# Sums of w_down in units of 256 columns, in two buffers, loaded by the SP queue

## The chip, the cores and the metric

The kernel runs on one core of one Trainium2 chip. The metric is the device time of one execution in microseconds (us), lower is better; the times shown are medians over several runs. One further execution was taken by the hardware profiler, and its trace is what this text reads. Engines: PE multiplies matrices (PEld loads its weights), DVE, ACT and POOL work on vectors, SP only issues transfers (DMAs). Each engine runs its instructions strictly in its own order; waits between engines, and for transfers, go through semaphores.

## The reference

One layer of a streaming encoder on x of 1024 positions by 1024 features, float32:

```python
h   = rmsnorm(x, norm1_g);  proj = h @ w_in                # q, k, v, forget logits, lru_x, lru_gate
att = forgetting_attention(q, k, v, cumsum(log f))         # 8 heads, causal
rec = rg_lru(conv(lru_x)) * gelu(lru_gate)
x   = x + concat(rmsnorm(att), rmsnorm(rec)) @ w_out
h2  = rmsnorm(x, norm2_g)
x   = x + (silu(h2 @ w_gate) * (h2 @ w_up)) @ w_down       # w_gate, w_up 1024x2816; w_down 2816x1024
```

The change touches the last line alone: the feed-forward part.

## The kernel before, in words

Float32 products are made of three products of split operands: `split` (L72 on ACT makes the high part h, L73 on DVE the low part l), and then h·h, h·l and l·h on PE.

The products with w_gate and w_up use a scheme with seven block products in place of eight. The work goes in 20 **steps**: gate step n and up step n for n = 1 to 10 (n = 0 is done with plain products before). This text calls them g1, u1, g2, u2 and so on. A step is seven **products** numbered 0 to 6, each of 12 matmuls (L936), so 140 products in all. `Step.run` gives products 0, 2, 4 and 6 the same PSUM bank (`x_`), products 1 and 5 another (`z_`), and product 3 a third (`w_`). Products 0, 1 and 2 are copied out by ACT (L1111). Then `result` adds: product 4 is added to the copy of product 1 by DVE, on L1104 in a gate step (`g<-Pg,pug`) and on L1099 in an up step (`puu<-Pu,puu`). Product 6 adds into the bank of product 4, so PE cannot begin it before DVE has read product 4. Between the two lies only product 5.

After each product a hook `after(i)` runs. It makes the operand of the next step that belongs to the same place (POOL sums L1068 to L1071 of raw weights, then `split`), and it carries the sums of w_down:

- `load_wd(f)` loads, for f = 0 to 10, four blocks of w_down (two blocks of rows, two halves of 512 columns each) into the tile `wd` of 128 x 4 x 512, in two transfers of 512 KB issued by ACT (L1019). There is one buffer under the tag `wd`.
- `sum_wd(f, m)`, m = 0 to 3, is one subtraction of 128x512 on DVE (L1025). After m = 3, SP stores the tile to `td[f]` in DRAM (1 MB, L1027). m = 0 reads only what the first transfer brought, m = 1 needs both.
- 13 products in the code are one turn: the load at place 0, the sums at places 7 to 10. The next load into the one buffer must wait until the store before it has landed.

The same tag `wd` is used before the steps by `t_sums` (four 512-column temporaries for every second of four sums). The raw weights of the steps come in pieces of 128x4x256 (512 KB, rows of 1 KB) on SP (`graw`, `uraw`, L901). SP also stores the results g (`gd`, L924) and their differences (`sd`, L928). The last part of the kernel (L1353, products P1 to P7) reads `td`, `sd` and `gd` back.

A scheduler of the framework puts the instructions of each engine into an order of its own, by its estimates of times. So what stands in an engine's order, not what stands in the code, says where a sum or a load comes.

Of the kernel before, what the change touches and what calls it, by code (L numbers as in the profile page):

```python
# [9 lines left out]
F32 = mybir.dt.float32  # L10
# [9 lines left out]
P = 128  # L20
# [14 lines left out]
def hymba_layer(ctx: ExitStack, tc: tile.TileContext, x, norm1_g, w_in, q_norm_g, k_norm_g, b_f,  # L35
# [5 lines left out]
    act, dve, pool, pe, sp = nc.scalar, nc.vector, nc.gpsimd, nc.tensor, nc.sync  # L41
# [18 lines left out]
    def bank(tag, name):  # L60
        return psp.tile([P, 512], F32, tag=tag, name=name, bufs=BANKS[tag])
# [3 lines left out]
    def any_bank(name, tags=("st", "st", "st", "o", "o", "mx")):  # L65
        cyc[0] += 1
        return bank(tags[cyc[0] % len(tags)], name)

    def split(src, h, l, gain=None):

        if gain is None:
            act.copy(out=h, in_=src)  # L72
            dve.tensor_sub(out=l, in0=src, in1=f32(h))  # L73
        else:
            act.activation(out=h, in_=src, func=AF.Copy, scale=gain)
            dve.scalar_tensor_tensor(out=l, in0=src, scalar=gain, in1=f32(h), op0=ALU.mult, op1=ALU.subtract)  # L76

    def rstd(out_t, ss, n, neghalf):

        dve.tensor_scalar(out=out_t, in0=ss, scalar1=1.0 / n, scalar2=EPS, op0=ALU.mult, op1=ALU.add)  # L80
        pool.tensor_tensor(out=out_t, in0=out_t, in1=neghalf, op=ALU.pow)
# [12 lines left out]
    def hs(half):  # L94
        return slice(half * 512, (half + 1) * 512)
# [212 lines left out]
    def sumsq_to_rstd(sq, dst, n, ps, b0=0, b1=NB):  # L308
        for b in range(b0, b1):
            pe.matmul(ps[:, b:b + 1], sq[:, b * P:(b + 1) * P], ones1[:, 0:1], start=True, stop=True)  # L310
        rstd_newton(dst[:, b0:b1], ps[:, b0:b1], n, b1 - b0)

    with tc.tile_pool(name="pp", bufs=1) as pp:
# [99 lines left out]
        for g, src in ((0, w_a), (1, w_x)):  # L413
            for o in range(2):
                sp.dma_start(out=wgr[o * HD:(o + 1) * HD, g, :, o * HD:(o + 1) * HD],
                             in_=src[0].rearrange("(t two) d e -> two d t e", two=2)[o])
# [437 lines left out]
    def mm_out(groups):  # L854

        for kc in range(4):
            wh, wl = woa[kc]
            for ps, b, half in groups:
                bh, bl = atth[kc][:, b * P:(b + 1) * P], attl[kc][:, b * P:(b + 1) * P]
                for m, (a, r) in enumerate(((bh, wh), (bl, wh), (bh, wl))):  # L860
                    pe.matmul(ps, a, r[:, hs(half)], start=(kc == 0 and m == 0), stop=(kc == 3 and m == 2))  # L861
# [35 lines left out]
    def load_raw(nm, n):  # L897
        src = w_gate if nm == "g" else w_up
        for j in range(2):
            raw = slot("v%d" % (2 * (nm == "u") + j), f"{nm}raw{n}{j}", F32, (P, 4, 256))  # L900
            sp.dma_start(out=raw, in_=src[0, j * 512:(j + 1) * 512, n * 256:(n + 1) * 256].rearrange("(k p) c -> p k c", p=P))  # L901
            raws[nm, j] = raw
# [16 lines left out]
    def g_tiles(n):  # L919
        gts[n] = [slot("x%d" % (2 * (n % 2) + i), f"g{n}{i}") for i in range(2)]  # L920
# [18 lines left out]
    def classic(nm, i, half, ops):  # L939
        ps = any_bank(f"c{nm}{i}{half}", A4)  # L940
        for j in range(2):
            product(ps, ops[nm, i, j], B[j, half], j == 0, j == 1)
        g = gts[0][i][:, hs(half)]
        if nm == "g":
            act.activation(out=g, in_=ps, func=AF.Silu)
        else:
            dve.tensor_mul(out=g, in0=g, in1=ps)
# [3 lines left out]
    def classic_ops(i):  # L951
        for nm in "gu":
            for j in range(2):
                ops0[nm, i, j] = make_op(blk(nm, i, j), f"c{nm}{i}{j}")

    with tc.tile_pool(name="nz", bufs=1) as nz:
        g2 = nz.tile([P, D], F32, name="g2")
        sp.dma_start(out=g2, in_=norm2_g[0:1, :].broadcast_to([P, D]))
        for b in range(4, NB):
            sp.dma_start(out=x1[b], in_=x1d[b * P:(b + 1) * P, :])  # L960
        x2d = dr.tile([S, D], F32, name="x2d")

        def norm2_block(b):
            xn = nz.tile([P, D], F32, tag="xn", name=f"x2n{b}", bufs=1)
            act.activation(out=xn, in_=x1[b], func=AF.Square, accum_out=ss2[:, b:b + 1])
            rstd(rs2[:, b:b + 1], ss2[:, b:b + 1], D, neghalf[:, 0:1])
            dve.scalar_tensor_tensor(out=xn, in0=x1[b], scalar=rs2[:, b:b + 1], in1=g2, op0=ALU.mult, op1=ALU.mult)
            ts = slice((b % 4) * P, (b % 4 + 1) * P)
            for kg in range(4):
                ps = any_bank(f"t2{b}{kg}", A4)  # L970
                for j in range(2):
                    kc = kg * 2 + j
                    pe.transpose(ps[:, j * P:(j + 1) * P], xn[:, kc * P:(kc + 1) * P], ident)
                h, l = (t[kg % 2][:, :, ts] for t in B[kg // 2, b // 4])
                split(ps[:, :256].rearrange("p (k t) -> p k t", k=2), h, l)

        for b0, nb in ((0, 2), (2, 1), (3, 1), (4, 1), (5, 1), (6, 1), (7, 1)):
            groups = [(any_bank(f"wa{b}{half}", B4), b, half) for b in range(b0, b0 + nb) for half in range(2)]
            mm_out(groups)
            if b0 in (0, 3):  # L980
                sumsq_to_rstd(sqA, rsA, AW, bank("tr", f"ssA{b0}"), *((0, 4) if b0 == 0 else (4, 8)))
            for ps, b, half in groups:
                dve.scalar_tensor_tensor(out=x1[b][:, hs(half)], in0=ps, scalar=rsA[:, b:b + 1], in1=x1[b][:, hs(half)], op0=ALU.mult, op1=ALU.add)
            for b in range(b0, b0 + nb):
                sp.dma_start(out=x2d[b * P:(b + 1) * P, :], in_=x1[b])
            for b in ((0, 1) if b0 == 2 else (b0 - 1,) if b0 else ()):
                norm2_block(b)
            if b0 == 5:
                load_raw("g", 0)
                load_raw("u", 0)  # L990
            if b0 == 6:
                classic_ops(0)
        g_tiles(0)


        seq = ("o1 g00 N7 ta0 g10 rw tb0 ta1 g11 tb1 ta2 g01 tb2 ta3 mk0 u00 tb3 mk1 u01 mk2 u10 sp0 mk3 mk4 u11 mk5 sp1 "
               "mk6 wd0").split()
        i7 = seq.index("N7")
        for q in seq[:i7]:
            classic_ops(1) if q == "o1" else classic(q[0], int(q[1]), int(q[2]), ops0)  # L1000
        norm2_block(7)

    tz = ctx.enter_context(tc.tile_pool(name="tz", bufs=1))

    def temp(name):
        return tz.tile([P, 512], F32, tag="sf", name=name, bufs=4)


    ND = NFT // 2
    TD = {"T1": 0, "T3": 1, "T4": 2, "T2": 3}  # L1010
    td = dr.tile([ND, P, 4, 512], F32, name="td")
    sd = dr.tile([ND, P, 512], F32, name="sd")
    wds = {}

    def load_wd(f):
        wds[f] = wd = tz.tile([P, 4, 512], F32, tag="wd", name=f"wd{f}", bufs=1)
        for i in range(2):
            rows = slice((ND * i + f) * P, (ND * i + f + 1) * P)
            act.dma_start(out=wd[:, 2 * i:2 * i + 2, :], in_=w_down[0, rows, :].rearrange("p (j c) -> p j c", j=2))  # L1019

    def sum_wd(f, m):

        wd = wds[f]
        o, a, b = ((0, 1, 0), (1, 3, 1), (3, 3, 0), (2, 2, 3))[m]
        dve.tensor_sub(out=wd[:, o, :], in0=wd[:, a, :], in1=wd[:, b, :])  # L1025
        if m == 3:
            sp.dma_start(out=td[f], in_=wd)  # L1027

    T1 = slots4("q", "T1")
    T2 = slots4("k", "T2")  # L1030
# [8 lines left out]
    def t_sums(k):  # L1039

        if k % 2 == 0:
            t = tz.tile([P, 4, 512], F32, tag="wd", name=f"ts{k}", bufs=1)
            u = [t[:, i, :] for i in range(4)]
        else:
            u = [temp(f"ts{k}{i}") for i in range(4)]
        for i, blk_ in enumerate((B11, B12, B21, B22)):
            h, l = ck(blk_, k)
            dve.tensor_add(out=u[i], in0=f32(h), in1=f32(l))
        for o, x_, y_ in ((0, 1, 0), (1, 3, 1), (3, 3, 0), (2, 2, 3)):
            dve.tensor_sub(out=u[o], in0=u[x_], in1=u[y_])  # L1050
        tsum[k] = u
# [199 lines left out]

    for k, st in enumerate(steps):
        def after(i):
            f, m = divmod(7 * k + i + 1, 13)
            if 0 <= f < ND:
                if m == 0:
                    load_wd(f)
                elif 7 <= m < 11:
                    sum_wd(f, m - 7)
            if k + 1 < len(steps):  # L1260
                steps[k + 1].make(i)
            else:
                end_step(i)
        if st.n + 1 < NPR:
            load_raw(st.nm, st.n + 1)
        st.run(after)
# [34 lines left out]
    for n, (nm, a_, b_, pos) in enumerate(dsteps):  # L1301
# [16 lines left out]
        if nm == "P6" and 7 <= pos < 11:  # L1318
            b = pos - 7
# [19 lines left out]
        if nm == "P4" and 4 <= pos < 8:  # L1339
            b = pos - 4  # L1340
# [8 lines left out]
        for b in range(4):  # L1349
# [9 lines left out]
            u = at({"P1": x2t[0, 0], "P2": x2t[0, 0], "P3": val.get("a"), "P7": val.get("q"), "P4": val.get("q")}[nm], b)  # L1359
# [30 lines left out]
```

## Time and profile before

| | us |
|---|---|
| median of three runs | 1179.3 (1174.34, 1179.3, 1183.54) |
| the profiled execution | 1176.27 |
| its span, first to last instruction | 1174.5 |
| PE busy in it | 1140.3 |
| the 20 steps in it, 566.21 to 961.23 | 395.02 |

The profiled execution is 1.77 us longer than its span, and 3.0 us below the median. Its row groups stand below under "Rows read from the trace". Times in them are us from the start of the span. A window row lists its stretch, its length, the busy time of the engine with the instructions in brackets, the granted clock as a share of full speed, the share of the DMA engines' time, and GB/s. A timeline row lists start, length, engine, line, operation, what is written and read, and in square brackets how long the engine stood idle before it and what ended that.

### The profile page before, as it was taken

To read this page: it belongs to the slowest core of one execution; us is meant where nothing else is said; L and a number is where in the kernel's file an instruction comes from. 1 tells how busy PE (TensorE), PEld (TensorE's weight loads), DVE (VectorE), ACT (ScalarE), POOL (GpSimd) and SP (SyncE) were. 2 spreads that over 40 slices of the span, in tenths; PEclk is the share of its full clock that TensorE was granted. 3 is DMA by queue.
4 is the path that set the end of the run, shared out by engine and by line. 5 is a ranking of instruction groups with operands and counts; after the bars stand their busy time and mean duration, and the time that the engine had idled before them with its cause. 6 is when DMAs were issued, how large, how long until landed. Compare 5 with 4: busy or idle time off the path is not lost.

```text
span 1174.5 us, 16494 instructions
## 1 busy us (share of the span) xinstructions
PE 1140.3 (97%) x6137; PEld 966.3 (82%) x6137; DVE 764.4 (65%) x1309; ACT 526.1 (45%) x951; POOL 174.5 (15%) x152
## 2 busy tenths in 40 slices
PE   8999999998999898999989999999999999999998
PEld 7988999996888786778868878888888888888887
DVE  6436858768787875779666665654433446679693
ACT  7427766326464554454333323333333334444442
POOL 2000010012010202000522223232222100000000
PEclk9999999999999999999999999999999999999999
DMA  6021111135666567541447554633223389842320
GB/s 251 20 56 53 38 37 37 30 73 118 167 150 153 148 154 212 190 151 55 147 177 267 197 194 182 214 102 106 83 61 96 125 320 337 280 145 95 99 82 36
DMA packets 94922, 159.70 MB, mean 136 GB/s; under 512 B 13105, under 2 KB 56217, under 8 KB 93434
## 3 DMA queue, kind: packets, MB, share of 16 engines
q1 hardware_dynamic: 91674, 147.11, 40.4%
q10 hardware_dynamic: 3168, 11.54, 2.8%
q8 instruction: 48, 0.79, 0.3%
q14 instruction: 32, 0.26, 0.1%
HBM read 103.41 MB, written 38.63 MB: 121 GB/s over the span
## 4 chain that ended last, share of the span: by engine, by line
PE 75%; DVE 10%; DMA 9%; issue 2%; ACT 2%; POOL 1%; SPq 0%; ACTq 0%; DVEq 0%; POOLq 0%
PE P L1353 18%; PE Pg L936 11%; PE Pu L936 11%; PE pag L361 4%; PE pbk L377 4%; PE pbv L377 4%; PE pax L361 4%; PE o L698 4%; PE pbq L377 4%; DMA td<-wd 3%; DMA wd<-in_w_down_dram 3%; PE fl L783 3%; DVE wd L1025 2%; PE wa L861 2%; PE mx L284 1%
## 5 line engine op out<-in xcount | busy, mean ns | idle before, releaser
L684 ACT ACTIVATE pt<-st 128x512 f32<-128x512 f32 (+1 forms) x96 | 47.9, 507 | 51.4 <-PE st L679 26.3
L1025 DVE TENSOR_TENSOR wd<-wd 128x512 f32<-128x512 f32 x44 | 43.9, 997 | 30.2 <-DMA wd<-in_w_down_dram 29.8
L689 DVE TENSOR_TENSOR ringl<-pt,ringh 128x512 fp32r<-128x512 f32 (+2 forms) x96 | 57.8, 616 | 7.7 <-ACT ringh L686 6.3
L287 DVE TENSOR_REDUCE nm<-mx 128x1 f32<-128x512 f32 (+2 forms) x96 | 51.3, 551 | 10.9 <-PE mx L286 6.6
L783 PE MATMUL fl<-worec,rech 128*128 128x256 f32 x256 | 52.5, 287 | 1.4 <-DVE ql L76 0.7
L783 PEld LDWEIGHTS fl<-worec,rech 128*128 128x128 f32 x256 | 42.0, 190 | 3.8 <-ACT worec L72 1.2
L1104 DVE TENSOR_TENSOR g<-Pg,pug 128x512 f32<-128x512 f32 x30 | 20.7, 689 | 30.8 <-PE Pg L936 30.8
L676 PE MATMUL st<-set 128*128 128x512 f32 (+1 forms) x96 | 35.5, 372 | 3.4 <-ACT pt L684 3.4
L698 PE MATMUL o<-ringl,vh 128*128 128x512 f32 (+1 forms) x96 | 34.7, 362 | 3.2 <-DVE ringl L689 3.2
L698 PE MATMUL o<-ringh,vh 128*128 128x512 f32 (+1 forms) x96 | 37.6, 392 | 0.0
L783 PE MATMUL fl<-worec,recl 128*128 128x256 f32 x128 | 36.1, 282 | 0.0
L1099 DVE TENSOR_TENSOR puu<-Pu,puu 128x512 f32<-128x512 f32 x30 | 20.7, 689 | 22.7 <-PE Pu L936 22.7
L698 PE MATMUL o<-ringh,vl 128*128 128x512 f32 (+1 forms) x96 | 34.1, 355 | 0.3 <-POOL vl L650 0.3
L1106 ACT ACTIVATE g<-g 128x512 f32<-128x512 f32 x30 | 19.0, 632 | 31.6 <-DVE g L1104 21.0
L1068 POOL TENSOR_TENSOR S1g<-graw,graw 128x512 f32<-128x512 f32 x10 | 15.1, 1514 | 103.1 <-DVE T L73 34.5
L480 POOL TENSOR_TENSOR sqR<-sqR,i 128x1024 f32<-128x1024 f32 x3 | 7.2, 2396 | 150.8 <-ACT i L479 150.8
L650 POOL TENSOR_TENSOR vl<-vn,vh 128x256 fp32r<-128x256 f32 x16 | 12.2, 772 | 111.7 <-ACT vh L649 111.7
L284 PE MATMUL mx<-set,qms 67*128 67x512 f32 (+2 forms) x72 | 25.5, 382 | 2.5 <-DVE nm L287 2.1
L435 DVE SCALAR_TENSOR_TENSOR xc<-xr,vcol,xc 128x1023 f32<-128x1023 f32 (+2 forms) x12 | 15.4, 1281 | 18.5 <-ACT xc L433 18.4
L686 ACT CAST ringh<-pt 128x512 fp32r<-128x512 f32 (+1 forms) x48 | 26.4, 549 | 1.6 <-PE o L698 0.8
L861 PE MATMUL wa<-wah,atth 128*128 128x512 f32 x64 | 25.8, 403 | 0.8 <-ACT wah L72 0.8
L688 DVE CAST ringh<-pt 128x384 fp32r<-128x384 f32 (+2 forms) x48 | 21.1, 440 | 6.7 <-ACT pt L684 6.4
(2172 smaller groups left out, 3983.8 us busy)
## 6 DMA issues: line engine op xcount, KB each, us to landing
graw<-in_w_gate_dram SPq DMA_DIRECT2D x22, 512.0 KB
uraw<-in_w_up_dram SPq DMA_DIRECT2D x22, 512.0 KB
wd<-in_w_down_dram ACTq DMA_DIRECT2D x22, 512.0 KB
gd<-g SPq DMA_DIRECT2D x22, 512.0 KB
td<-wd SPq DMA_DIRECT2D x11, 1024.0 KB
xt<-in_x_dram SPq DMA_DIRECT2D x8, 512.0 KB
set<-qh SPq DMA_DIRECT2D x16, 256.0 KB
xp<-in_x_dram SPq DMA_DIRECT2D x32, 128.0 KB
```

What stands on the lines that cost most here:

```text
L284: pe.matmul(ps[:, :w], qm[:67, qb * P:(qb + 1) * P], kb[:67, j0 * P:j0 * P + w], start=True, stop=not diag)
L287: dve.tensor_reduce(out=nm[:, ch * 8 + qb:ch * 8 + qb + 1], in_=ps[:, :nk], axis=AX.X, op=ALU.max, negate=True)
L361: pe.matmul(ps[g][:, :n], a, r, start=(kc == 0 and m == 0), stop=(kc == KC - 1 and m == 2))
L377: pe.matmul(ps[g][:, :n], a, r, start=(kc == 0 and m == 0), stop=(kc == KC - 1 and m == 2))
L684: act.activation(out=pt[:, off:], in_=ps[:, off:], func=AF.Exp)
L689: dve.tensor_sub(out=pl[:, off:], in0=pt[:, off:], in1=f32(ph[:, off:]))
L698: pe.matmul(ot[:, off:], a[:, j * VW:j * VW + P], r[:, off:], start=(j == 0 and m == 0), stop=(j == jmax and m == 2))
L783: pe.matmul(ps[:, :256], a, r, start=(n == 0), stop=(n == 11))
L861: pe.matmul(ps, a, r[:, hs(half)], start=(kc == 0 and m == 0), stop=(kc == 3 and m == 2))
L936: pe.matmul(ps, a[:, k, :], chunk(b, k), start=first and m == 0, stop=last and m == 11, skip_group_check=more)
L1025: dve.tensor_sub(out=wd[:, o, :], in0=wd[:, a, :], in1=wd[:, b, :])
L1353: pe.matmul(ps, x_[:, bs], y_, start=(begin and m == 0), stop=(end and m == 2))
```

## The change

The sums go in 22 units q of 256 columns (f = q // 2, which half of each 512 is q % 2) instead of 11 of 512. The tile is 128 x 4 x 256, half as large, and there are two buffers, in the same space. The loads move from ACT to SP. A unit's load stands three products ahead of a multiple of six (`6*q-3`), its four sums at `6*q+4` to `6*q+7`, so that in the code the load of q comes seven products before its first sum. Units 0 and 1 are loaded before the steps. The store of a unit goes to 256 of each 512 columns of `td`. `t_sums` gets its four temporaries as two tiles of the new size.

```diff
-               "mk6 wd0").split()
+               "mk6 wd0 wd1").split()
...
-    def load_wd(f):
-        wds[f] = wd = tz.tile([P, 4, 512], F32, tag="wd", name=f"wd{f}", bufs=1)
+    def load_wd(q):
+
+        f, cs = q // 2, slice((q % 2) * 256, (q % 2 + 1) * 256)
+        wds[q] = wd = tz.tile([P, 4, 256], F32, tag="wd", name=f"wd{q}", bufs=2)
         for i in range(2):
             rows = slice((ND * i + f) * P, (ND * i + f + 1) * P)
-            act.dma_start(out=wd[:, 2 * i:2 * i + 2, :], in_=w_down[0, rows, :].rearrange("p (j c) -> p j c", j=2))
+            sp.dma_start(out=wd[:, 2 * i:2 * i + 2, :], in_=w_down[0, rows, :].rearrange("p (j c) -> p j c", j=2)[:, :, cs])
-    def sum_wd(f, m):
+    def sum_wd(q, m):
-        wd = wds[f]
+        wd = wds[q]
         o, a, b = ((0, 1, 0), (1, 3, 1), (3, 3, 0), (2, 2, 3))[m]
         dve.tensor_sub(out=wd[:, o, :], in0=wd[:, a, :], in1=wd[:, b, :])
         if m == 3:
-            sp.dma_start(out=td[f], in_=wd)
+            sp.dma_start(out=td[q // 2][:, :, (q % 2) * 256:(q % 2 + 1) * 256], in_=wd)
...
-            t = tz.tile([P, 4, 512], F32, tag="wd", name=f"ts{k}", bufs=1)
-            u = [t[:, i, :] for i in range(4)]
+            t = [tz.tile([P, 4, 256], F32, tag="wd", name=f"ts{k}{i}", bufs=2).rearrange("p (a b) c -> p a (b c)", a=2) for i in range(2)]
+            u = [t[i // 2][:, i % 2, :] for i in range(4)]
...
-            f, m = divmod(7 * k + i + 1, 13)
-            if 0 <= f < ND:
-                if m == 0:
-                    load_wd(f)
-                elif 7 <= m < 11:
-                    sum_wd(f, m - 7)
+            e = 7 * k + i
+            for q in range(2 * ND):
+                if e == 6 * q - 3 and q >= 2:
+                    load_wd(q)
+                elif 0 <= e - (6 * q + 4) < 4:
+                    sum_wd(q, e - 6 * q - 4)
```

The order changes in three places that the next sections speak of. The first is DVE in g1, around the additions of products 3 and 4 (`g10` and `g11`); au10l to au16l are low parts of the operands of u1. Before:

```order
L73 TENSOR_TENSOR au12l_6363<-S2u1_6321,au12h_6362 128x512
L1104 TENSOR_TENSOR g10_6305<-Pg12_6302,pug10_6303 128x512
L73 TENSOR_TENSOR au13l_6381<-uraw11_6026,au13h_6380 128x512
L1104 TENSOR_TENSOR g11_6306<-Pg10_6300,pug10_6303 128x512
L73 TENSOR_TENSOR au14l_6399<-S3u1_6322,au14h_6398 128x512
L1025 TENSOR_TENSOR wd1_6564<-wd1_6564 128x512
```

and now:

```order
L73 TENSOR_TENSOR au12l_6368<-S2u1_6326,au12h_6367 128x512
L1106 TENSOR_TENSOR g10_6310<-Pg12_6307,pug10_6308 128x512
L73 TENSOR_TENSOR au13l_6386<-uraw11_6027,au13h_6385 128x512
L1027 TENSOR_TENSOR wd2_6511<-wd2_6511 128x256 x3
L1106 TENSOR_TENSOR g11_6311<-Pg10_6305,pug10_6308 128x512
L73 TENSOR_TENSOR au14l_6405<-S3u1_6327,au14h_6404 128x512
```

The first sums of the second load stood behind the addition of product 4 (`g11`); now three sums of unit 2 stand ahead of it.

The second is SP at the same time, from the loads of raw weights in g1 on. Before (the loads of wd1 and wd2 stand on ACT):

```order
L901 DMA graw21_6298<-in_w_gate_dram 128x4x256
L901 DMA uraw20_6438<-in_w_up_dram 128x4x256
L1027 DMA td_5972<-wd0_6293 128x2048
L1027 DMA td_5972<-wd1_6564 128x2048
L901 DMA uraw21_6440<-in_w_up_dram 128x4x256
L901 DMA graw30_6592<-in_w_gate_dram 128x4x256
```

and now:

```order
L901 DMA graw21_6303<-in_w_gate_dram 128x4x256
L901 DMA uraw20_6445<-in_w_up_dram 128x4x256
L1029 DMA td_5972<-wd0_6295 512x1x256
L1029 DMA td_5972<-wd1_6298 512x1x256
L1021 DMA wd2_6511<-in_w_down_dram 128x2x256 x2
L1021 DMA wd3_6651<-in_w_down_dram 128x2x256 x2
L1029 DMA td_5972<-wd2_6511 512x1x256
L1029 DMA td_5972<-wd3_6651 512x1x256
```

The loads of units 2 and 3 stand directly behind the stores of units 0 and 1, whose buffers they take.

The third is DVE in g2, from the addition of product 3 (`g20`) on; g3 and g4 repeat it with units 14, 15 and 20, 21. Before:

```order
L1104 TENSOR_TENSOR g20_6601<-Pg22_6598,pug20_6599 128x512
L73 TENSOR_TENSOR au23l_6677<-uraw21_6440,au23h_6676 128x512
L1104 TENSOR_TENSOR g21_6602<-Pg20_6596,pug20_6599 128x512
L73 TENSOR_TENSOR au24l_6695<-S3u2_6618,au24h_6694 128x512
L1104 TENSOR_TENSOR g20_6601<-Pg21_6597,pug21_6600 128x512
```

and now:

```order
L1106 TENSOR_TENSOR g20_6611<-Pg22_6608,pug20_6609 128x512
L73 TENSOR_TENSOR au23l_6692<-uraw21_6447,au23h_6691 128x512
L1027 TENSOR_TENSOR wd8_7302<-wd8_7302 128x256
L1106 TENSOR_TENSOR g21_6612<-Pg20_6606,pug20_6609 128x512
L73 TENSOR_TENSOR au24l_6711<-S3u2_6628,au24h_6710 128x512
L1027 TENSOR_TENSOR wd8_7302<-wd8_7302 128x256
L1027 TENSOR_TENSOR wd9_7431<-wd9_7431 128x256
```

One sum of unit 8 now stands ahead of the addition of product 4 (`g21`). The last sums of all stand in g4 now (units 20 and 21); before, those of wd10 stood in u5.

## Rows read from the trace of the kernel before

**Rows 1.** The page, parts 1: span, and busy time of PE.

```profile
span 1174.5 us, 16494 instructions
PE 1140.3 (97%) x6137; PEld 966.3 (82%) x6137; DVE 764.4 (65%) x1309; ACT 526.1 (45%) x951; POOL 174.5 (15%) x152
```

**Rows 2.** Windows, PE: steps g1, u1, u3, then u4's end to the last step.

```profile
566.21:585.25 19.04, 19.04 (x86) 1.00 0.57 198
585.25:612.42 27.17, 21.57 (x85) 0.94 0.46 155
...
669.94:693.72 23.78, 21.23 (x86) 0.93 0.48 172
...
732.75:961.23 228.48, 228.48 (x1009) 1.00 0.39 129
sum 395.02, PE 386.14; mean PE 42.90
```

**Rows 3.** Timeline of PE: first matmuls behind its three longest waits; g4 begins.

```profile
594.18 0.86 PE L936 MATMUL Pu<-T,au12h 128*128 128x512 f32 x2 [3.33 <-ACT puu L1111]
...
609.56 0.50 PE L936 MATMUL Pu<-T4hB,au16h 128*128 128x512 f32 x1 [2.11 <-DVE puu L1099]
...
689.27 0.50 PE L936 MATMUL Pu<-T4hB,au36h 128*128 128x512 f32 x1 [2.42 <-DVE puu L1099]
...
693.72 0.63 PE L936 MATMUL Pg<-B,ag40h 128*128 128x512 f32 x2
```

**Rows 4.** Timeline of ACT in g1 and u1.

```profile
586.11 0.63 ACT L1106 ACTIVATE g<-g 128x512 f32<-128x512 f32 x1 [8.43 <-DMA td<-wd]
```

**Rows 5.** Timeline of SP: transfers issued in g1, g3, g4 and g5.

```profile
576.50 0.40 SPq L901 DMA_DIRECT2D graw<-in_w_gate_dram  x1
...
577.75 17.69 SPq L1027 DMA_DIRECT2D td<-wd  x2
...
660.28 0.45 SPq L1027 DMA_DIRECT2D td<-wd  x1
...
700.36 0.45 SPq L1027 DMA_DIRECT2D td<-wd  x1
...
741.00 0.47 SPq L1027 DMA_DIRECT2D td<-wd  x1
```

**Rows 6.** Windows: clock, DMA share and GB/s, raw loads alone, then the store; g1 to u4.

```profile
577.50:581.50 4.00, 4.00 (x19) 1.00 0.94 241
581.50:584.30 2.80, 2.80 (x14) 1.00 1.04 425
664.30:667.00 2.70, 2.70 (x14) 1.00 1.02 424
564.00:720.00 156.00, 147.74 (x631) 0.98 0.58 201
```

**Rows 7.** The chain that ended last: start, length, what.

```profile
577.75 7.83 DMA td<-wd
...
660.28 7.71 DMA td<-wd
...
668.01 3.54 DMA wd<-in_w_down_dram
```

**Rows 8.** Timelines of DVE and PE: addition of product 4 in g1, start of product 6.

```profile
580.01 0.69 DVE L1104 TENSOR_TENSOR g<-Pg,pug 128x512 f32<-128x512 f32 x1 [0.35 <-PE Pg L936]
...
582.53 0.39 PE L936 MATMUL Pg<-T4hB,ag16h 128*128 128x512 f32 x1
```

**Rows 9.** DVE groups by form (busy us, mean ns, idle before); DVE busy from 564 to 760.

```profile
L1025 DVE TENSOR_TENSOR wd<-wd 128x512 f32<-128x512 f32 x44 | 43.9, 997 | 30.2 <-DMA wd<-in_w_down_dram 29.8
...
L73 DVE TENSOR_TENSOR B<-t,B 128x256 fp32r<-128x256 f32 x16 | 5.6, 417 | 3.2 <-ACT B L72 3.2
...
564.00:760.00 196.00, 126.14 (x170) 0.98 0.58 199
```

**Rows 10.** Window behind PE's wait of 3.33 us: PE busy, then clock.

```profile
594.00:598.00 4.00, 3.82 (x10) 0.58 0.58 197
```

## The prediction

> **What bounds the kernel now.** I read the page first: PE is busy for 1140.3 of 1174.5 us [rows 1], so only time that PE spends waiting can be won. Next come the windows of the 20 steps. A step in which PE never waits lasts 19.04 us (g1), one product so 2.72 us; from u4's end on all twelve steps together take 228.48 = 12 x 19.04 [rows 2]. The 20 steps take 395.02 us instead of 380.8, so 14.2 us are lost in them: 8.1 in u1 (27.17), 4.7 in u3 (23.78), 1.4 elsewhere [rows 2]. That is the most this change can win there.
>
> Then the timeline of PE says what each loss is. In u1 PE waits 3.33 us for a copy by ACT (`puu`) and 2.11 us for DVE; in u3 2.42 us for DVE [rows 3]. The first comes from ACT: it stood idle for 8.43 us until the store `td<-wd` had landed [rows 4], because its next instruction was the load into the one buffer of `wd`, and the Silu and the copies stood behind it. DVE for its part idles 29.8 us in total before sums whose load has not landed [rows 9]. So a wait of a transfer, on either engine, becomes a wait of PE wherever something that PE needs within a product stands behind it.
>
> A wait costs more than its length. After the 3.33 us the granted clock averages 0.58 of full speed for 4 us, partly at the lower of the two levels, 1.2 against 2.4 GHz [rows 10]. Behind the 2.42 us product 6 of u3 takes from 689.27 to 693.72, 4.45 us for 2.72: 1.73 lost on top. Behind the 2.11 us product 6 takes 609.56 to 612.42, or 0.14 more [rows 2, 3]. I price 1.73 for a wait of 2.4 us or more, nothing below.
>
> **What the change removes.** ACT issues no transfer any more, so its 8.43 us and the copy that came late for PE go. The largest part of the 8.1 us in u1 has this cause. The waits on DVE do not go by themselves: the sums still stand in its order, and what they wait for still runs in a ring of store, load, sums, store. The order of SP shows that the lead of seven products is not there: the load of units 2 and 3 stands directly behind the stores of units 0 and 1, and must wait until these have landed, since it takes their buffers. What is late next is therefore a sum on DVE.
>
> **What it adds: transfers.** Pieces of w_down and `td` are now 1 KB long instead of 4 and 8 KB. No row shows a store or a load of w_down in 1 KB pieces. The raw weights come in 1 KB pieces, and while only they run, the engines are 0.94 busy and move 241 GB/s; the store in 8 KB pieces behind them moves 425 [rows 6]. For loads I take 241 (same direction, same piece). For stores the ends are 241 and 425: 512 KB take 2.17 or 1.23 us; both rows are equally near, so 1.7. The fixed part of a transfer follows from a load of 512 KB that lands after 3.54 us [rows 7]: less 1.24 us at 424 GB/s [rows 6] it is 2.30, of which I put 1.15 ahead of the data and 1.15 behind.
>
> The Trainium skill, "Perfetto Trace Analysis", section "DMA Optimizations", has rules for both sides. One says that small transfers under 2 KB carry much overhead each and should be batched: it speaks against this change, and rows 6 agree. The other says that smaller transfers may start sooner where the engines are mostly idle: the share is 0.58 over the stretch [rows 6]. By the first alone the result is the second rival below, by the second alone the first.
>
> **Term 1, g1.** On DVE three sums of unit 2 now stand ahead of the addition of product 4. Before, that addition began at 580.01, at once when PE was done, and product 6, which needs it, at 582.53 [rows 8]. Now: raw loads fill the queue until 581.5 [rows 6], the store of unit 0 is issued at 577.75 as before [rows 5], its data run 581.5 to 583.2, it has landed at 584.35. The load's data start at 585.5 (the store of unit 1 ended at 584.9), two halves of 1.09 us each end at 587.7, the second has landed at 588.83. Two sums of 0.42 us each (the 128x256 form [rows 9]) and the addition of 0.69 [rows 8] end at 590.36. PE waits from 582.53: 7.8 us (7.4 to 8.3 with the two store rates), with the clock 9.6.
>
> **Term 2, g2, g3 and g4.** In each of them one sum (units 8, 14, 20) stands ahead of the addition of product 4. Let T be the start of the gate step; product 6 is due at T + 6 x 2.72 = T + 16.32. The store that the load follows was issued before at T + 6.64 in g4 (700.36 against 693.72) and T + 8.25 in g5 (741.00 against 732.75) [rows 2, 3, 5], behind the raw loads. Now three sums of the pair before stand ahead of the addition of product 5 in the up step, with a load of their own to wait for, and everything behind them up to the store slips: I take T + 9. In g3 the raw data ran until 664.3, 4.0 us after the store's issue at 660.28 [rows 5, 6]. Then 1.7 of store and 1.15 to land: T + 15.85; load 1.15 + 1.09 + 1.15: T + 19.24; sum 0.42 and addition 0.69: T + 20.35. PE waits 4.0 us, with the clock 5.8. Three times: 17.3. The ends are an issue at T + 6.64 (wait 1.7, no slow clock) and one at T + 12 (7.0 + 1.73), if the up steps slip as much again.
>
> **Parts at nothing.** DVE does 88 sums of 0.42 us (36.7) for 44 of 997 ns (43.9 [rows 9]); it is busy 126 of 196 us there, so the sums cost only where they stand ahead of an addition. SP issues 44 loads and 22 stores for 11 stores, at about 0.4 to 0.5 us each [rows 5], and mostly waits anyway; behind its waits stand raw loads, which are used more than a step later. If that cover is gone, POOL's sums and with them whole operands are late, which is the second rival. `t_sums` keeps its instructions. The last part of the kernel keeps its order, and its first tiles of `td` are stored earlier than before.
>
> **Sum.** 9.6 + 17.3 = 26.9 us lost in the steps instead of 14.2, so 12.7 more. Against the profiled execution: 1176.3 + 12.7 = 1189.0; against the median of the runs, 3.0 higher, 1192.0. I say 1190. With all low ends (7.4 + 1.73 + 3 x 1.7 = 14.2) nothing changes: 1176; with all high ends (8.3 + 1.73 + 3 x 8.7 = 36.1) it is 1198.
>
> **Rivals.**
>
> 1. *The ring keeps pace: not slower.* Place: the store ahead of g2, g3 and g4. It decides from an issue at T + 7 or earlier, where PE waits less than 2.1 us and the clock stays. For it: before, T + 6.64 occurred; a unit is half as large, so it lands sooner, and ACT brings its copies on time. Against it: three rounds of store and load now fit into two steps, where before nine rounds took 741.00 - 577.75 = 163 us, 18.1 each [rows 5]. Time: 9.6 + 3 x 1.7 or less, 9.6 to 14.7 lost: 1171.6 to 1176.8 by the profile.
>
> 2. *The transfers become the bound: slower by more.* Per two steps, three pairs of units move 3 x 2.1 MB, 26.1 us at 241 GB/s; four raw loads 2.1 MB, 8.7 us; `gd` and `sd` 1.6 MB, 3.7 us at 424. That is 38.5 us in 38.08. SP stands still for each landing, so the queue cannot be filled either: with two fixed parts of 2.30 us a round of 12.8 us becomes some 16. The order places ten rounds between g1 and the end of product 5 of g4, 43 products or 117 us; at 16 they take 160, 43 lost, 28.8 more than before: 1205. For it: the rates of rows 6. Against it: the stores may run at 425, and 18.1 us per round before was with other work in between, so it proves no floor.
>
> 3. *All of it is won.* Neither ACT nor DVE holds PE: 1176.3 - 14.2 = 1162. This needs loads well ahead of their sums, which the order does not have; the change then does not do what its numbers in the code say.
>
> **How the numbers follow.** Forecast 0.48 (its own range 1183 to 1197), first rival 0.23, second 0.24, third 0.05. The range for eight in ten reaches from within the first rival to the middle of the second: 1173 to 1206. About 1% (12 us) is what a measurement of this kernel tells from no change. Faster by more than that is the third rival alone: 0.05. Slower by more are the second rival and a little over half of the forecast, which lies near the bound: 0.50. The rest, 0.45, lies within.
>
> **What would show each step.** In the timeline of PE in g1: a wait of 7 to 9 us ahead of product 6, ended by DVE's addition (`g`, now L1106), and on DVE ahead of it an idle time ended by the load of `wd`. In g2 to g4: a wait of 2 to 7 us at the same place. ACT shows no idle time ended by `td`. DMA windows with stores of 1 KB pieces at 240 to 425 GB/s. No wait in the steps after g4. It is wrong if PE waits under 4 us in g1, if the waits in g2 to g4 sum to under 3 us, or if steps after g4 lose time.

## The result: slower by 1.15%, and the profile after

The median of four runs is 1194.09 us (1185.65 to 1196.34), that of the kernel before in the same comparison 1179.37 (1174.34 to 1183.54). The ratio over the runs is 1.0115, its 95% interval 1.0089 to 1.014 (the two medians alone give 1.0125). So it is slower, by about what I had called the bound of a measurement; 1190 and "slower" were forecast. The profiled execution took 1192.11 us with a span of 1190.3, 15.8 more than the one before.

Where it went is read from the windows of PE by step (the counterpart of [rows 2]): g1, u1, g2 and so on to u4, then the twelve steps from g5 to u10 in one.

```profile
566.41:594.24 27.83, 20.93 (x85) 0.88 0.57 192
594.24:613.86 19.62, 19.35 (x85) 1.00 0.69 219
613.86:640.79 26.93, 21.76 (x85) 0.88 0.60 201
640.79:661.00 20.21, 19.46 (x85) 0.99 0.72 224
661.00:684.48 23.48, 20.51 (x85) 0.95 0.68 223
684.48:705.43 20.95, 19.76 (x85) 0.98 0.73 229
705.43:729.20 23.77, 20.67 (x85) 0.94 0.67 218
729.20:748.51 19.31, 19.31 (x85) 0.99 0.35 109
748.51:977.00 228.49, 228.49 (x1010) 1.00 0.36 116
```

The 20 steps take 410.59 us, 29.8 more than the 380.8 of steps without a wait; before they lost 14.2. Now the gate steps lose 25.9 and the up steps 3.9; before, nearly all of the loss was in up steps [rows 2]. The stretches ahead of them (566.4 us) and behind them (213.3) are as long as before (566.2 and 213.3), so all of the change lies in the steps. What PE waits for there, from its timeline in g1 and g2 (the wait is in brackets):

```profile
589.80 0.80 PE L936 MATMUL Pg<-T4hB,ag16h 128*128 128x512 f32 x1 [6.90 <-DVE g L1106]
635.51 0.79 PE L936 MATMUL Pg<-T4hB,ag26h 128*128 128x512 f32 x1 [5.17 <-DVE g L1106]
```

In g3 and g4 it is 2.97 and 3.10 us at the same place. In the sum of all waits (us in total, times, longest) this is one row, with the up steps' in the other:

```profile
PE Pg L936 <- DVE g L1106: 18.1, 4, 6.9
...
PE Pu L936 <- DVE puu L1101: 2.2, 3, 1.2
```

DVE in g1 shows what held it. Its addition for PE stands behind three sums, the first of which waits for its load:

```profile
579.45 0.68 DVE L73 TENSOR_TENSOR au13l<-uraw,au13h 128x512 fp32r<-128x512 f32 x1
587.53 0.42 DVE L1027 TENSOR_TENSOR wd<-wd 128x256 f32<-128x256 f32 x1 [7.41 <-DMA wd<-in_w_down_dram]
588.26 0.89 DVE L1027 TENSOR_TENSOR wd<-wd 128x256 f32<-128x256 f32 x2 [0.30 <-DMA wd<-in_w_down_dram]
589.06 0.68 DVE L1106 TENSOR_TENSOR g<-Pg,pug 128x512 f32<-128x512 f32 x1
```

And SP shows what the load waits for. Its timeline from g3 to g4, the issues of `td` and `wd` only:

```profile
669.58 1.25 SPq L1029 DMA_DIRECT2D td<-wd  x2
676.33 2.56 SPq L1021 DMA_DIRECT2D wd<-in_w_down_dram  x4
683.79 3.53 SPq L1029 DMA_DIRECT2D td<-wd  x2
...
688.05 1.76 SPq L1021 DMA_DIRECT2D wd<-in_w_down_dram  x2
...
690.50 1.28 SPq L1021 DMA_DIRECT2D wd<-in_w_down_dram  x2
696.99 3.73 SPq L1029 DMA_DIRECT2D td<-wd  x2
700.81 4.12 SPq L1021 DMA_DIRECT2D wd<-in_w_down_dram  x4
...
714.09 1.25 SPq L1029 DMA_DIRECT2D td<-wd  x2
```

Two stores go out together, the two loads for the same two buffers follow when they have landed, then the sums, then two stores again. The two buffers turn in step like one; no load leads. This text calls the time from one such pair of stores to the next a **round**, and the whole the **ring**. From 669.58 to 714.09 three rounds take 44.51 us, and the two steps from g3 to g4 (661.00 to 705.43) 44.43. The order gives three rounds, six units, to each two steps, so PE's two steps last as long as three rounds. In the chain that ended last, between 575 and 720 us, the loads of `wd` have 26.1%, the stores to `td` 25.1% and the sums 21.4%; the rest is other work of DVE and issuing, and PE has no part of note.

### The profile page after: what moved, and what is told of

Read it like the earlier page. It is cut to its first block, busy times and chain, and to the rows that moved or that the text cites. A ratio compares the mean times of both kernels' runs of the same rounds, so it can differ in the third digit from the quotient of the medians.

```text
span 1190.3 us, 16591 instructions
## 1 busy us (share of the span) xinstructions
PE 1147.5 (96%) x6137; PEld 972.8 (82%) x6137; DVE 772.0 (65%) x1353; ACT 528.3 (44%) x951; POOL 172.4 (14%) x152
## 4 chain that ended last, share of the span: by engine, by line
PE 74%; DVE 12%; DMA 9%; issue 2%; ACT 2%; POOL 1%; SPq 1%; DVEq 0%; POOLq 0%; ACTq 0%
PE P L1355 17%; PE Pu L936 11%; PE Pg L936 10%; PE pag L361 4%; PE pbk L377 4%; PE pbv L377 4%; PE pax L361 4%; PE o L698 4%; PE pbq L377 3%; DMA wd<-in_w_down_dram 3%; DMA td<-wd 3%; PE fl L783 3%; DVE wd L1027 3%; PE wa L861 2%; DMA rb<-rd 2%
## 5 line engine op out<-in xcount | busy, mean ns | idle before, releaser
L1027 DVE TENSOR_TENSOR wd<-wd 128x256 f32<-128x256 f32 x88 | 54.0, 632 | 45.2 <-DMA wd<-in_w_down_dram 43.7
L435 DVE SCALAR_TENSOR_TENSOR xc<-xr,vcol,xc 128x1023 f32<-128x1023 f32 (+2 forms) x12 | 15.4, 1280 | 18.5 <-ACT xc L433 18.4
L861 PE MATMUL wa<-wah,atth 128*128 128x512 f32 x64 | 25.9, 405 | 0.2 <-ACT wah L72 0.2
L783 PEld LDWEIGHTS fl<-worec,recl 128*128 128x128 f32 x128 | 25.3, 198 | 0.6
```

The costliest lines, as they stand in the source:

```text
L783: pe.matmul(ps[:, :256], a, r, start=(n == 0), stop=(n == 11))
```

## The experiments

The stretch ahead of g1 differs by up to 4.4 us between the profiled executions (g1 began at 566.2 to 570.7), even where its instructions and their order are the same: before and before with the sums held mark the two ends. So next to the median I give the length of the 20 steps in the profile, less 380.8: what the steps **lost**. It comes from one execution of each kernel. Each ratio is to runs of the kernel before in the same comparison, whose medians were 1178.9 to 1181.23.

| kernel | median us | ratio to before, 95% | steps lost, us |
|---|---|---|---|
| before | 1179.37 | | 14.2 |
| changed | 1194.09 | 1.0115 (1.0089 to 1.014) | 29.8 |
| before, loads by SP | 1176.95 | 0.9983 (0.9965 to 1.0001) | 11.2 |
| changed, loads by ACT | 1196.58 | 1.0137 (1.0103 to 1.0172) | 33.9 |
| changed, sums of four units behind product 4's addition | 1182.66 | 1.0037 (1.002 to 1.0055) | 21.1 |
| changed, store in 4 KB pieces | 1187.97 | 1.0072 (1.0044 to 1.01) | 27.5 |
| changed, sums held at their places | 1162.94 | 0.9862 (0.9838 to 0.9886) | 0.0 |
| before, sums held at their places | 1163.98 | 0.9873 (0.9846 to 0.99) | 0.0 |
| held, a unit every 4 products | 1164.03 | 0.9866 (0.9836 to 0.9895) | 0.0 |
| held, every 3 | 1167.72 | 0.9895 (0.9865 to 0.9925) | 3.8 |
| held, every 2 1/3 | 1174.0 | 0.9951 (0.9933 to 0.9969) | 10.0 |
| the same, half stores | 1165.1 | 0.9866 (0.9839 to 0.9893) | 1.4 |

**The change taken apart: the queue.** Each kernel with its loads moved to the other queue.

```diff
-            act.dma_start(out=wd[:, 2 * i:2 * i + 2, :], in_=w_down[0, rows, :].rearrange("p (j c) -> p j c", j=2))
+            sp.dma_start(out=wd[:, 2 * i:2 * i + 2, :], in_=w_down[0, rows, :].rearrange("p (j c) -> p j c", j=2))
```

In the kernel before (loads now by SP):

> The kernel before with one word changed: its loads of w_down are issued by SP in place of ACT; units of 512 columns, one buffer, order left to the scheduler. If each part of the change is judged by itself: ACT no longer stops for the store (8.43 us in g1), the copy that came 3.33 us late in u1 comes on time, and the scheduler does not put more than one sum ahead of an addition that PE needs at once; the steps lose 5 to 11 us in place of 14.2, the time is 1167 to 1176. Rival (moving the wait into SP's queue is what costs in the changed kernel, since stores and raw weights stand behind it there): the steps lose 20 us or more, the time is 1185 or more.

And the reverse in the changed kernel (loads again by ACT):

> The changed kernel with one word changed back: its loads are issued by ACT, units of 256 columns in two buffers and their places in the code stay. Theory A (units and buffers let the scheduler pack sums too early on DVE; the queue is not the cause): the waits ahead of product 6 in g1 to g4 stay, and ACT's wait for the store comes on top, as before the change; the time is 1192 to 1206. Rival (SP's queue is the cause): loads no longer hold SP, stores go out earlier, the waits of PE fall under 9 us in total; the time is 1183 or less.

The four numbers form a square. The queue of SP saves 3.0 us of loss with the old units (14.2 to 11.2) and 4.1 with the new ones (33.9 to 29.8). Units and buffers cost 19.7 and 18.6. So the rival that made SP's queue the cause falls. That the queue was a small gain rests on one execution each: by the medians neither pair can be told apart. Both expectations missed something: before with SP's loads lost 11.2, just more than the 5 to 11 expected, and with ACT's loads in the changed kernel the waits did not stay at their places (g4 loses 0.3 there, u2 5.1 and u3 7.5).

In the kernel before with SP's loads ACT no longer stops for the store, and yet u1 loses 8.09 us, as it did with ACT's loads (8.13). The copy for PE is still late (PE waits 2.13 us for it in u1, and 3.89 for DVE ahead of product 6). DVE and ACT there:

```profile
593.00 0.69 DVE L1025 TENSOR_TENSOR wd<-wd 128x512 f32<-128x512 f32 x1 [7.68 <-DMA wd<-in_w_down_dram]
593.61 0.68 DVE L1104 TENSOR_TENSOR g<-Pg,pug 128x512 f32<-128x512 f32 x1
...
594.32 0.63 ACT L1106 ACTIVATE g<-g 128x512 f32<-128x512 f32 x1 [7.12 <-DVE g L1104]
```

ACT waits for DVE, whose addition stands behind a sum that waits for its load. The trace of the kernel before has the same at this place, 5.39 us behind the row of [rows 4]:

```profile
590.18 0.69 DVE L1025 TENSOR_TENSOR wd<-wd 128x512 f32<-128x512 f32 x1 [2.19 <-DMA wd<-in_w_down_dram]
590.79 0.68 DVE L1104 TENSOR_TENSOR g<-Pg,pug 128x512 f32<-128x512 f32 x1
...
591.50 0.63 ACT L1106 ACTIVATE g<-g 128x512 f32<-128x512 f32 x1 [3.20 <-DVE g L1104]
```

So already before the change the last wait ahead of the late copy was for a sum, and not ACT's stop of 8.43 us for the store.

**Only the sums ahead of one addition.** `add4[n]` is the addition of product 4 in gate step n; the edge fixes an order on DVE and adds no wait.

```diff
+        n = {2: 1, 8: 2, 14: 3, 20: 4}.get(q)
+        if n:
+            tc.add_manual_dep(ins.ins, add4[n].ins.name, mybir.DependencyInfo(mybir.DependencyClass.NoSync, mybir.DependencyReason.DATA), reason="place")
```

> The changed kernel, with the sums of units 2, 8, 14 and 20 held behind the addition of product 4 of g1, g2, g3 and g4 in DVE's order; queue, units, buffers and transfers stay. Theory A (PE waits because those sums stand ahead of that addition, while the ring of store and load has room): the four waits of PE of 6.90, 5.17, 2.97 and 3.10 us ahead of product 6 go, the steps lose 4 to 14 us instead of about 30, the time is 1168 to 1180. Theory B (the transfers in pieces of 1 KB are too slow for the pace, wherever the sums stand): the same time is lost a step later, in the up steps, ahead of products that need DVE's additions there; the time stays above 1186.

It came out between the two. All four waits ahead of product 6 of the gate steps are gone, as theory A has it; but four new ones stand in the up steps, where theory B looked for them: 4.36 us in u1 for ACT's copy, and 3.42, 2.39 and 3.36 ahead of product 6 of u1, u2 and u3. DVE and ACT in u1 say why:

```profile
593.88 1.48 DVE L1028 TENSOR_TENSOR wd<-wd 128x256 f32<-128x256 f32 x4 [2.44 <-DMA wd<-in_w_down_dram]
595.28 0.68 DVE L1110 TENSOR_TENSOR g<-Pg,pug 128x512 f32<-128x512 f32 x1
...
596.00 0.63 ACT L1114 ACTIVATE g<-g 128x512 f32<-128x512 f32 x1 [9.35 <-DVE g L1110]
```

The sums now stand ahead of the next addition, that of product 5; the Silu waits for that, and the copy for PE behind the Silu. So theory A as I had it, one place in the order, is too narrow: what is late meets the next addition.

**All sums at their places in the code.** `latest` lists DVE's last operation of each result as the code writes them (the addition in a gate step, the multiplication in an up step; the lines that fill it are not shown). A sum may not come ahead of the last of these that is written ahead of it. Nothing else changes in the code.

```diff
-        dve.tensor_sub(out=wd[:, o, :], in0=wd[:, a, :], in1=wd[:, b, :])
+        ins = dve.tensor_sub(out=wd[:, o, :], in0=wd[:, a, :], in1=wd[:, b, :])
+        if latest:
+            tc.add_manual_dep(ins.ins, latest[-1].ins.name, mybir.DependencyInfo(mybir.DependencyClass.NoSync, mybir.DependencyReason.DATA), reason="place")
```

> The changed kernel, with every sum of w_down held in DVE's order behind the last addition of the steps that the code has ahead of it, so that the sums stand where the code puts them and a load leads its sums by some seven products (19 us). Theory A: a load lands long before its sums, DVE never idles before a sum for long, no step loses more than 1 us, the time is 1160 to 1167. Theory B: store, load and raw weights do not get through in six products (16.3 us) per unit; DVE idles before the sums still, waits of PE of 2 us and more remain, the time is 1180 or more.

The whole loss is gone, with the same transfers in the same 1 KB pieces on the same queue. The edges set the pace too: the last sum began at 729.9 us in the changed kernel and begins at 928.0 now. The window of all 20 steps, and the row of the sums:

```profile
566.78:947.58 380.80, 380.80 (x1681) 1.00 0.51 166
```

```profile
L1028 DVE TENSOR_TENSOR wd<-wd 128x256 f32<-128x256 f32 x88 | 61.1, 695 | 0.9
```

DVE idles 0.9 us before sums, where it was 45.2 in the changed kernel and 30.2 before [rows 9]; PE is busy in every microsecond of the steps. Sums still stand directly ahead of additions here. With their data landed that costs PE nothing.

The same lines in the kernel before, with its 512 columns, one buffer and ACT's loads:

> The kernel before (512 columns, one buffer, loads issued by ACT), with every sum held in DVE's order behind the last addition that the code has ahead of it. Theory A, with the place of the sums as the whole cause: the load comes three products (8 us) after the store in the code and seven ahead of its sums, so ACT waits under 1 us and DVE not at all; the time is 1160 to 1168, and units, buffers and queue of the change are worth nothing beside it. Its rival (the queue matters by itself): ACT still stops for the store to land, copies come late, u steps lose 2 to 4 us each in two or more places; the time is 1170 to 1178.

```profile
570.65:951.48 380.83, 380.83 (x1682) 1.00 0.47 164
```

Again nothing is lost, and the two medians differ by less than their intervals. Once the sums are held, units, buffers and queue are worth nothing that these runs can tell. (ACT still idles 6.7 us in total for `td` ahead of copies there, more than the 1 us expected, and no copy comes late for PE.)

**The pace.** With the sums held, the pace can be set. `6 * q` becomes `4 * q` and `3 * q`, with the load at `4 * q + 1` and `3 * q + 2`. The lead of a load ahead of its sums shrinks with the pace, from seven products to three and two.

> The kernel with all sums held at their places in the code, but a unit every 4 products (10.9 us) in place of 6, its load 3 products ahead of its sums in place of 7. If the ring of store and load takes 10 to 14 us per buffer (fixed parts 2 x 2.3, data 1.7 and 2.2, sums 1.7 to 2.5, raw weights in the way), two buffers allow one unit in 5 to 7 us: nothing is late, the time is 1161 to 1166. If the pieces of 1 KB or SP's queue allow less, DVE idles before sums and PE waits by 2 us and more in several steps: 1170 or more.

> The same with a unit every 3 products (8.2 us), its load only 2 products (5.4 us) ahead of its sums; the order of the changed kernel packs 20 units into about 55 products, 2.8 products each. If that pace is what the ring cannot keep, sums are late here as in the changed kernel: DVE idles 20 us or more before sums, PE waits in several steps, the time is 1172 to 1190. If instead a sum's place ahead of an addition is all, whatever the pace, then 1161 to 1166 as with 6 and 4 products.

At 4 products DVE idles 5.2 us before sums, at 3 it is 20.5, and only there PE waits, 1.82 us in g3. That is under what I expected of a pace too fast, and over what place alone would give. So I asked for the pace that the scheduler's order asks for (the calls between these lines are left out):

```diff
-                if e == 6 * q - 3 and q >= 2:
+                s = 7 * q // 3 + 4
+                if q >= 2 and e == 7 * (q - 2) // 3 + 8:
...
-                elif 0 <= e - (6 * q + 4) < 4:
+                if 0 <= e - s < 4:
```

> All sums held no earlier than their places in the code, but a unit every 2 1/3 products (6 units in the 14 products of a gate and an up step, 6.35 us each, as the order of the changed kernel packs them), its load right behind the store that frees its buffer. Ring theory (the time of one round of store, load and sums of two units, 14.8 to 15.4 us in the changed kernel from store to store, against 12.7 us that the order gives it, is what PE waits for): the steps lose some 20 x (7.5 - 6.35) = 23 us, 15 to 30 with what is hidden at the start and the clock; the time is 1177 to 1193. Place theory (only sums that the scheduler drew ahead of one addition hurt, whatever the pace): the steps lose under 7 us, as with 3 products per unit; the time is 1163 to 1170.

Again between the two: 10.0 us. A load leads its sums by no product or one here. What sets the loss shows in the profile. PE waits once in two steps, ahead of product 6 of u2, u3 and u4:

```profile
643.33 0.50 PE L936 MATMUL Pu<-T4hB,au26h 128*128 128x512 f32 x1 [2.26 <-DVE puu L1104]
...
685.29 0.54 PE L936 MATMUL Pu<-T4hB,au36h 128*128 128x512 f32 x1 [1.97 <-DVE puu L1104]
...
726.91 0.51 PE L936 MATMUL Pu<-T4hB,au46h 128*128 128x512 f32 x1 [1.65 <-DVE puu L1104]
```

These lie 41.96 and 41.62 us apart. SP's stores of the same six units:

```profile
625.76 3.87 SPq L1032 DMA_DIRECT2D td<-wd  x2
...
668.05 3.87 SPq L1032 DMA_DIRECT2D td<-wd  x2
...
709.74 3.86 SPq L1032 DMA_DIRECT2D td<-wd  x2
```

42.29 and 41.69: three rounds of 14.0 (the expectation took 14.8 to 15.4), where the order gives 12.7 (38.08 for three). PE goes at the ring's pace.

**The store's share of the round.** The same kernel with half of each store left out (the last part then reads the stored blocks twice; that edit is not shown):

```diff
-            sp.dma_start(out=td[q // 2][:, :, (q % 2) * 256:(q % 2 + 1) * 256], in_=wd)
+            sp.dma_start(out=td[q // 2][:, :2, (q % 2) * 256:(q % 2 + 1) * 256], in_=wd[:, :2, :])
```

> The kernel with a unit every 2 1/3 products, and only two of the four blocks of a unit stored (256 KB in place of 512 KB; blocks 2 and 3 of td are left out, the last part reads blocks 0 and 1 in their place, as many bytes). If the data time of the stores is a fair part of the round, as my 1.7 us per 512 KB says, a round of two units gets 1.7 us shorter (1.2 to 2.2) and the loss falls by about 10 x 1.7 = 17 us of the 23 expected in full; the steps lose 4 to 12 us, the time is 1166 to 1175. If the fixed parts and SP's turns are the round, the loss stays within 5 us of that of the full stores.

The loss falls by 8.6 of 10.0 us, to less than I expected, and six units now take 38.15 and 38.75 us (stores at 627.12, 665.27 and 704.02): the ring is hardly slower than PE any more. The leads in the code are as short as with full stores, so they alone do not cost the 10.0 us. Shorter stores win nearly all of it back: that the round of store, load and sums is the bound at this pace is thereby shown.

**Larger pieces in the store.** A unit's store goes to a layout of its own, the reading back changes with it.

```diff
-    td = dr.tile([ND, P, 4, 512], F32, name="td")
+    td = dr.tile([ND, 2, P, 4, 256], F32, name="td")
...
-            sp.dma_start(out=td[q // 2][:, :, (q % 2) * 256:(q % 2 + 1) * 256], in_=wd)
+            sp.dma_start(out=td[q // 2, q % 2], in_=wd)
```

> The changed kernel, with td in DRAM laid out so that a unit's store goes out in pieces of 4 KB in place of 1 KB; the last part reads td back in pieces of 1 KB in place of 2 KB. Sums, order, loads as in the changed kernel. My term of the store (512 KB take 1.7 us at 1 KB pieces, 1.23 us in large ones): each round gets 0.5 us shorter, 0.9 at most, the four waits in g1 to g4 shrink by 0.5 to 1 us each, the time is 1188 to 1192. Rival (the pieces of 1 KB are what makes the ring slow): stores land 2 us or more earlier, the waits fall by half, 1182 or less. If reading back in smaller pieces costs, PE waits in the last part, which it does not now.

Nine rounds take 131.9 us (579.41 to 711.29), 14.65 each, where the changed kernel needs 135.9 (578.22 to 714.09), 15.1. That is 0.45 us less per round, near the 0.5 expected, and 2.3 us less lost. The four waits did not all shrink: they are 7.39, 3.86, 2.24 and 3.42 us, so those of g1 and g4 grew. Pieces of 1 KB in the store are not what makes the ring slow; those of the loads were left as they are, and no run changes them.

## Why the prediction was right, and where it was not

**The direction and the size** were right for the reasons given in the two terms: no lead, since a load must wait for the store from its own buffer, and sums ahead of additions. 29.8 us are lost where 26.9 were summed. In part that is luck: rates taken too low made the forecast waits too long, a price of the clock taken too low made the forecast loss too short.

**What the change removes.** Here a step failed. The prediction put the largest part of the 8.1 us lost in u1 down to ACT's stop of 8.43 us for the store. With that stop gone and nothing else changed (before, loads by SP) u1 loses 8.09 us: the sum ahead of DVE's addition had been the last wait there all along.

**Term 1, g1.** 6.90 us for 7.8 (7.4 to 8.3). Step by step: the load could be issued at 584.48 (I said 584.35); the second sum began at 588.26 (588.83); the addition ended at 589.74 (590.36). The rates were too low. The windows while stores run, and while loads run (here the number behind the length is the granted clock, then the share of the DMA engines and GB/s):

```profile
582.00:583.00 1.00, 1.00 1.09 384
583.00:584.00 1.00, 1.00 1.08 382
...
587.00:588.00 1.00, 0.50 0.95 312
588.00:589.00 1.00, 0.50 0.94 301
```

Stores in 1 KB pieces move some 383 GB/s, 1.37 us per 512 KB and not 1.7; loads some 300, not 241. The rule that the prediction cites from the Trainium skill, "Perfetto Trace Analysis", section "DMA Optimizations", speaks of transfers under 2 KB; those here are of 256 and 512 KB, in pieces of 1 KB, and for stores the piece changes the rate little (383 against 425 [rows 6]). In the last two rows the granted clock is 0.50, the lower of its two levels (1.2 GHz), while PE waits. With the clock g1 and u1 lost 9.37 us (9.6).

**Term 2, g2 to g4.** The stores were issued at T + 9.62, 8.58 and 8.66 (I took 9), the waits are 5.17, 2.97 and 3.10 (4.0 each). g2 and u2 lost 9.06, g3 and u3 6.35, g4 and u4 5.00: 20.4 for 17.3. Two things were mis-sized. Waits of 0.75 and 1.19 us in u2 and u3 were not in the sum. And the clock: less all waits the rest is 3.14, 2.19 and 1.90, where I put 1.73. I had read that price from one wait; rows 2 and 3 hold a dearer case, since the 8.13 us lost in u1 less its waits of 3.33 and 2.11, and the 0.14 behind the second, leave 2.55 behind the first.

**The other step that failed is a reason, not a number:** I fixed the store's issue within a step and let the rest follow, and set the ring against it as a rival that costs 28.8 us more than before at 16 us a round (its own parts, 12.8 and two fixed parts of 2.30, give 17.4). They are one mechanism. A round took 15.1, the order asked for 12.7, and each two steps lasted three rounds. In the kernel before, the stores of g3, g4 and g5 [rows 5] are 40.1 and 40.6 us apart with one in each up step between, so one unit of 512 columns had a whole step of 19.04 us or more, for a round that took 18.1 in the mean. After the change the round of 512 columns was 3 us shorter (before, other work lay in between, so 18.1 is no measure of the ring alone), and the order asked for it 6.3 us sooner.

**Parts at nothing.** ACT has no idle time ended by `td`, and the steps after g4 have no wait: u4 loses 0.27 us, the twelve behind it nothing (228.49 for 228.48). The 88 sums took 54.0 us and not 36.7 (why, the last section says). Where they took 61.1, no step lost anything, so on DVE there was room for them; in the ring of the changed kernel they count.

**The third rival,** all of it won at 1162, is what the change does once its places in the code are held: 1162.94. I was right that the order did not have the lead, and the sums held back show that the order, with the pace that it sets, was all that stood in the way.

**Still open** is how the 29.8 us divide. By these runs some 10 may come with the pace (2 1/3 products, held, lose 10.0). In the kernel with four units moved, g2 to u10 lose 9.7 (that is 21.1 less the 11.4 of g1 and u1), where the changed kernel loses 20.4: about 10.7 for sums ahead of the gate steps' additions. The remaining 9 to 11 are g1 and u1, where the first units come with no lead. These three were not run one by one. Nor were units and buffers: no run has the small units in one buffer, or the large ones in two.

## What to carry to other kernels

A lead written into the code is worth only what stands in the engine's order; where a scheduler draws work ahead, look there, and hold it with an order-only edge if it must stay. Compare the round of a ring (store, load, work, from store to store) with the time that the order gives it: here two buffers that turn in step shortened the round of the same data little, and the order asked for it sooner. And a wait that is moved, to another engine or to another place on the same one, meets the next thing that the critical engine needs.

## What was not expected of the hardware

A sum of 128x256 takes 0.42 us alone and 1.5 us beside an addition on POOL. From the kernel with the sums held, DVE:

```profile
601.43 1.52 DVE L1028 TENSOR_TENSOR wd<-wd 128x256 f32<-128x256 f32 x1
...
604.68 1.51 DVE L1028 TENSOR_TENSOR wd<-wd 128x256 f32<-128x256 f32 x1
```

and POOL:

```profile
600.99 1.68 POOL L1075 TENSOR_TENSOR S3u<-uraw 128x512 f32<-128x512 f32 x1 [4.20 <-DVE ag24l L73]
604.30 1.60 POOL L1076 TENSOR_TENSOR S4u<-uraw,S2u 128x512 f32<-128x512 f32 x1 [1.62 <-DVE ag25l L73]
```

POOL's additions end at 602.67 and 605.90, the sums that began inside them at 602.95 and 606.19, each 0.28 or 0.29 later. In the whole trace 28 of the 88 sums begin inside an instruction of POOL, and 27 of these end 0.28 or 0.29 us after it; the other 60 take 0.41 to 0.43 us, also where POOL begins during them. So a sum seems to wait until POOL is done. The Trainium skill, "SBUF — State Buffer", section "SBUF: two separate sides", has a rule that fits: a DVE operation with two SBUF inputs and a GpSimd operation that reads SBUF want the same pair of ports, and the one that starts first holds it for its whole instruction. The rows agree. It explains the mean of 695 ns for a median of 422. In the kernel with the sums held it cost PE nothing. In the changed kernel nine such sums, of 1.41 to 1.52 us, stand in the chain that ended last, between 590 and 709 us, for instance:

```profile
707.54 1.44 DVE wd L1027
```

Each is about 1 us longer than a sum alone, so over nine rounds this is about 1 us of the 15.1 us round. It is an estimate from these rows; no run takes it out.
